# A planned hybrid-decoder kernel: three Strassen-like pairs for four, room behind GpSimd's results, and remainders spread anew

## The chip, the cores and the metric

The kernel runs on one core of a Trainium2 chip, as one launch. The metric is the device time of one execution in microseconds (us). The kernel before was timed three times: 726.03, 728.19 and 728.18 us, a median of 728.18 us. In the profile the engines are PE (TensorE, matmuls), PEld (its weight loads), DVE (VectorE), ACT (ScalarE), POOL (GpSimd) and SP (SyncE, which here only issues transfers).

## What is computed

One decoder layer on 1024 tokens of width 1024, in fp32 (the reference, cut to what matters):

```
mod = silu(c) @ mod_w + mod_b;  shift, scale, gate = split(mod, 3)
h = rmsnorm(x) * (1 + scale) + shift
u = h @ w_in                                  # 1024 x 5120
cv, cg, cs, lx, ls = split(u, 5)              # 1024 columns each
v = causal_depthwise_conv(cv * sigmoid(cg), dw_w, 31 taps)
y_conv = (silu(layernorm(v)) @ pw2_w + pw2_b) * silu(cs)
xs = causal_depthwise_conv(lx, sc_w, 4 taps)
r, i = sigmoid(block_diagonal(xs, wr) + br), sigmoid(block_diagonal(xs, wi) + bi)
a = exp(-8 r softplus(-lam))
hs = scan(h = a h + sqrt(1 - a^2) i xs)       # along the tokens
y_lru = hs * silu(ls)
x = x + (1 + gate) * (concat(y_conv, y_lru) @ w_out)
return rmsnorm(x)
```

## The kernel before

**Tiles.** Everything lies transposed: 128 channels on the partitions, 1024 tokens along the free axis, so that one tile of 128 x 1024 is one of 8 k-tiles of the input or one of 40 column tiles of w_in (i0 to i39 in the tables: conv value, conv gate, conv SiLU gate, lru x, lru gate, 8 each). An fp32 matmul is made of three matmuls of a rounded format: each operand is split into a high part (a cast on ScalarE: whi of weights, uh of tokens) and a remainder (raw minus the high part: wlo, ul), and H x H, H x remainder and remainder x H are summed in PSUM. A column tile is thus 8 k-tiles x 3 terms x 2 halves of 512 tokens = 48 matmuls of 512 columns.

**Who makes a remainder** can be chosen: a subtraction on DVE, one on POOL, or "by transfer": ScalarE writes the negated high part, and an accumulating transfer, which POOL issues, adds the original from memory (the function remainder: ACT, then ADD). For the weights the choice stands in EARLYD, EARLY and LATE (function weights), for the pairs in DENG and WSUB (function duo), for the lru group's result y in YDMA (function gates).

**Pairs.** A slot "iA+iB" of the table ORDER is a pair (function duo, tiles dn and up in PSUM): on four of the eight k-tiles the two column tiles are taken together and computed in the Strassen-Winograd manner, with 7 quarter products for 8. For this the pair needs combinations of its weights (tile wz, four operations of 128 x 256 each, on the engine CSUB, split into wsh and wsl), and sums of the tokens (function token_sums: hx on POOL, split into hhs, by ScalarE, and hls, by POOL), which are made once, before the first pair.

**Stages.** First four column tiles while the input norm is found; then the mixing stage (slots up to 39: a column tile or a pair each, between them the block-diagonal products "gate"; on DVE, ScalarE and GpSimd's transfers the 31 taps of the convolution, on DVE and ScalarE the gates and the scan); slots 40 to 47 the product of the lru group with its half of w_out, also in pairs; then layer norm, the pw2 product, the other half of w_out, the residual and the last norm.

**What sets the order.** A planner (class Plan) takes every operation with an engine, a cost, a priority (mostly the slot number plus or minus something) and what it reads and writes, plays the engines forward in time, and so fixes for each engine one order in which its instructions stand in the program. On the chip each engine goes through its order and waits in place. The planner knows that a DVE operation on two SBUF operands and a POOL operation exclude each other (its "held" times), and counts a latency from an operation's end to its reader (LATENCY: 0.15 us for POOL). Buffers come from a pool of 47 tiles of 128 x 1024 ("big") and are handed on, so that an operation may also wait for the last reader of a buffer's former content. The modulation product is made on DVE: tiles modw of mod_w are multiplied and summed by scalar_tensor_tensor (line 458 of the profile).

**Transfers.** SP issues loads of raw weights and others from its own queue (q1 in the profile), POOL the accumulating ones from another (q0). The residual x is copied from memory to memory (accd <- in_xT, nine transfers) from the slot XCN on, so that later transfers can add to it.

Lines that the prediction names: 439 (ScalarE copies and casts), 447 (ScalarE activations), 458 (scalar_tensor_tensor), 466 (tensor_tensor on DVE or POOL), 471 (POOL's accumulating transfers), 485 (SP's transfers), 599 (matmuls of a column tile), 1329 (gate), 1678 (quarter products of a pair).

Of the kernel before, what the change touches and what calls it, by code (L numbers as in the profile page):

```python
# [31 lines left out]
FIRST = (("in", CG), ("in", CV), ("in", CG + 1), ("in", CV + 1))  # L32
FW = len(FIRST) * P
NEXT = (("in", LS), ("in", CS), ("in", CS + 1))
ORDER = "i10 i24 g0 i2 i25 i11 i3 i26 i33 i12 i4 g1 i34 i23 g2 i13 i35 i5 i27 i21 g3 i14 i19 i6 i36+i28 i15 i30+i37 i7 i29+i38 g4 g6 g5 i31 i39 i22+i18 g7 i20"
EW = FW + len(NEXT) * P
START = ((0, H), (H, T))
END = ((0, H), (H, 768), (768, T))
NBIG = 47
LASTK = 7  # L40
SPARE = 3
# [6 lines left out]
HRES = 0  # L48
POOLED = (1, 3)
TLATE = 3.0  # L50
QGATES = ((1, 5), (3, 0), (3, 2), (3, 4))
# [25 lines left out]
NP = {0: (6,), 512: (6, 0, 7), 768: (6, 0)}  # L77
SUMS = (2, 0, 4, 3, 1, 6, 7, 5)
CSD = 2
SPILL = (0, 2, 4, 6)  # L80
SPP0, SPP1, SPN = 30, 40.5, 41
EVN = 4
CQR = 0
# [5 lines left out]
KQ = -0.3  # L89
TSETS = 15  # L90
DUOA = 2
DUOW = "big"
YSP = (0, 1, 2, 3)
YRES = 5
TSP = 24
TRES = 2
TSUB = "POOL"
WSUB = ("POOL", "POOL", "POOL")
DENG = {14: ("DMA", "DVE", "DVE"), 15: ("POOL", "DMA", "DVE"), 16: ("DMA", "DVE", "POOL"), 17: ("DMA", "DVE", "DMA"), 18: ("POOL", "POOL", "DMA"), 19: ("DVE", "DVE", "POOL"), 20: ("POOL", "DVE", "POOL"), 21: ("DMA", "DMA", "POOL"), 22: ("DVE", "DVE", "DVE"), 23: ("POOL", "DVE", "POOL"), 24: ("POOL", "DVE", "DMA"), 25: ("POOL", "POOL", "DMA"), 26: ("POOL", "POOL", "POOL"), 27: ("POOL", "DMA", "POOL"), 28: ("POOL", "POOL", "DVE"), 29: ("DMA", "DVE", "DVE"), 30: ("DVE", "DVE", "DVE"), 32: ("POOL", "POOL", "POOL"), 34: ("DMA", "DVE", "DVE"), 35: ("DVE", "DVE", "DMA"), 36: ("POOL", "DMA", "DMA"), 37: ("POOL", "DVE", "DVE"), 38: ("DVE", "DVE", "DVE"), 39: ("DMA", "DVE", "DMA"), 40: ("DMA", "DMA", "DVE"), 41: ("DMA", "DMA", "POOL")}
YDMA = (3, 6, 7)  # L100
EVD = 0
DUOE = 1.2
CSUB = "POOL"
LACT = ((0, 0), (0, 1), (1, 0), (1, 1))
LORDER = "p1zy2q3s4r"
LORDERS = {}
# [1 line left out]
LTJ = (0.0, 0.4)  # L108
YORD = (0, 1, 2, 3, 4, 5, 6, 7)
LTDMA = ()  # L110
YSTEP = 0.3
LTD = (2,1)
PREN, PRES = 5, 3
PREP, XCP = 18, 19
PLAND = 6.0
XCN = 35
LEV = ()
LWB = "big"
LWO = 0.7
# [6 lines left out]
STORE_HOLD = ""  # L126
AFTER_ROOT = ((6, 768),)
FORKP = (1, 2, 3)
FORKN = -3.0
FEVD = ()  # L130
FEVN = 0.1
QT = {(0, c): ("HW", "X") for c in "y234"}
PLACED = ("big",)
MARGINS = 2.0
LSN = 1
LEVN = 0.7
# [4 lines left out]
LLATE = 45  # L141
SLOTT = {46: ("HX", "W"), 47: ("HX", "W")}
FINQ = 0.0
LRV = (0, 2, 4)
QRES = 3
SINGLE = (0,)
AHEAD = 4
IDLE, IDLE0 = 12, 4
WARM = (2, 1)
LANDING, MARGIN = 4.0, 2.0  # L150
BACKLOG = 6.0
SP0 = 1.0
# [3 lines left out]
GDOT = "DVE"  # L156
FOLD = "DVE"
EARLY = 18
EARLYD = (14, 28, 30, 31, 32, 33, 38, 40)
LATE, LAND = 41, 6.0  # L160
ISSUE, FLIGHT, RATE = 1.0, 10.0, 3.0
GM = 17
# [30 lines left out]
class Plan:  # L193
# [61 lines left out]
    def order(self):  # L255
# [139 lines left out]
def hymba_layer(ctx: ExitStack, tc: tile.TileContext, xT, vecs, mod_w, w_first, w_in,  # L395
# [31 lines left out]
    def d_cost(n, ptr=0):  # L427
        return 0.07 + 0.00104 * n + 0.06 * ptr
# [33 lines left out]

    def TT(prio, eng, out, a, b, op, n=T, r=(), w=(), reserve=0, after=()):
        e = dve if eng == "DVE" else pool
        return S.op(eng, d_cost(n) if eng == "DVE" else p_cost(n),
                    lambda: e.tensor_tensor(out=out(), in0=a(), in1=b(), op=op), prio, r, w,  # L466
                    reserve=reserve, lock=not in_psum(r), after=after)

# [115 lines left out]

    def weights(s, after=(), n=None, eng=None, where=None, late=(), later=()):
        n = number[s] if n is None else n
        eng = eng or ("DMA" if n in EARLYD or n >= LATE else "POOL" if n < EARLY else "DVE")
        w_bufs(s, where)
        w_slice(s, 0, KT, n - 2.5, n - 1.4, after, eng, late, later)

# [695 lines left out]
    def evac_in(m, ps, n, b=None, rb=(), ev=0.5):  # L1286
# [10 lines left out]
        elif kind == CS:  # L1297
            t = big_buf(f"scs{i}")
            ACT(pr, t, ps, AF.Silu, bias=b, r=[ps, *rb], w=[t])
            scs_d[i] = dram.tile([P, T], F32, tag=f"scs{i}", name=f"scsd{i}")  # L1300
            DMA(pr, lambda: scs_d[i], t, FULL_BYTES, r=[t], w=[("scsd", i)])
        elif kind == LS:
            sls[i] = big_buf(f"sls{i}", parts=2)
            return ACT(pr, sls[i], ps, AF.Silu, bias=b, r=[ps, *rb], w=[sls[i]])
        else:
            xs, xh, xl = (big_buf(f"{a}{i}", d) for a, d in
                          (("xs", F32), ("xsh", F32R), ("xsl", F32R)))

# [734 lines left out]
```

## Time and profile before

| what | before |
|---|---|
| median of three runs | 728.18 us |
| profiled execution | 728.47 us, its span 726.0 us |
| granted TensorE clock, mean | 0.994 |
| TensorE busy | 713.5 us (98%), 3244 matmul records |
| VectorE busy | 655.7 us (90%), 898 |
| ScalarE busy | 474.7 us (65%), 601 |
| GpSimd busy | 206.1 us (28%), 181 |
| transfers | 135.17 MB, mean 186 GB/s |

Views of the profile are read so. A row of engine waits is "engine, tile, line <- what it waited for: us in total, times, longest us". A row of windows gives the stretch, its length, and for PE, PEld, DVE, ACT and POOL the busy us with the count of instructions in brackets, then the granted clock, the share of the transfer engines' time and GB/s; a window asked for one engine and one tile has that one alone. A row of a timeline is start, duration, engine, line, operation, out <- in, shapes, and in square brackets how long the engine stood idle before it and what released it. A row of groups ends in "| busy us, mean ns | idle before, releaser". A row of transfers is out <- in, the issuing queue, the count, KB each, and the median us from issue to landing. Since TensorE is busy nearly always, the other engines matter only where it waits for them.

### The profile page before, as it was taken

The numbers are of one execution on the slowest core, as the hardware profiler recorded it, in microseconds if no ns is written. First come the engines' busy times: TensorE is split into PE (matmuls) and PEld (weight loads), VectorE is DVE, ScalarE is ACT, GpSimd is POOL, SyncE is SP. The second block draws the span as 40 slices with busy tenths as digits, with TensorE's granted clock in tenths as the row PEclk, the third lists the DMA queues.
The fourth block names the chain that finished last, engine by engine and source line by source line (L and its number), as shares of the span: only waits on it lengthen the run. The fifth ranks groups of instructions, "written<-read, shape, count | busy, mean of one in ns | idle before, by whom it ended". The sixth has DMA issues, their size and how long they took to land.

```text
span 726.0 us, 9074 instructions
## 1 busy us (share of the span) xinstructions
PE 713.5 (98%) x3244; PEld 593.0 (82%) x3244; DVE 655.7 (90%) x898; ACT 474.7 (65%) x601; POOL 206.1 (28%) x181
## 2 busy tenths in 40 slices
PE   9999999999989999999999999999999999999996
PEld 8888888888868888888888887878888888888885
DVE  7999999999988989989999999997798966999647
ACT  7650689657659974774676788846797635745322
POOL 0036334433955643075150230011101001100001
PEclk9999999999999999999999999999999999999998
DMA  8946438988788999868743466697947766774006
GB/s 335 407 157 191 65 98 227 233 249 202 179 188 215 240 220 219 216 174 172 169 109 76 152 210 177 221 311 199 259 87 156 185 151 136 234 187 178 30 1 232
DMA packets 44909, 135.17 MB, mean 186 GB/s; under 512 B 5073, under 2 KB 14545, under 8 KB 44753
## 3 DMA queue, kind: packets, MB, share of 16 engines
q1 hardware_dynamic: 27152, 88.95, 34.8%
q0 software_dynamic: 16704, 44.73, 34.4%
q10 hardware_dynamic: 1008, 0.92, 0.4%
q8 instruction: 25, 0.41, 0.2%
q14 instruction: 20, 0.16, 0.1%
HBM read 83.43 MB, written 25.17 MB: 150 GB/s over the span
## 4 chain that ended last, share of the span: by engine, by line
PE 76%; DVE 16%; issue 3%; ACT 3%; DMA 1%; DVEq 0%; POOL 0%; ACTq 0%; POOLq 0%
PE ps L599 25%; PE xout L775 6%; PE xpw L775 6%; PE first L908 5%; DVE caccs L458 5%; PE dn L1678 3%; PE up L599 3%; PE ypw L775 3%; PE lx L1478 3%; DVE xs L458 2%; PE dn L599 2%; DVE cacc L458 2%; PE gate L1329 2%; PE zout L775 1%; PE zpw L775 1%
## 5 line engine op out<-in xcount | busy, mean ns | idle before, releaser
L599 PE MATMUL ps<-uh,whi 128*128 128x512 f32 x448 | 139.1, 392 | 3.6 <-ACT r L447 3.6
L599 PE MATMUL ps<-uh,wlo 128*128 128x512 f32 x448 | 138.4, 390 | 0.0
L599 PE MATMUL ps<-ul,whi 128*128 128x512 f32 x448 | 138.3, 390 | 0.0
L599 PEld LDWEIGHTS ps<-uh,whi 128*128 128x128 f32 x448 | 84.3, 189 | 21.7 <-ACT r L447 4.0
L599 PEld LDWEIGHTS ps<-ul,whi 128*128 128x128 f32 x448 | 84.5, 189 | 17.7
L599 PEld LDWEIGHTS ps<-uh,wlo 128*128 128x128 f32 x448 | 84.4, 188 | 17.6
L439 ACT CAST whi<-raw 128x1024 fp32r<-128x1024 f32 (+1 forms) x44 | 44.3, 1011 | 39.0 <-PE ps L599 15.4
L466 POOL TENSOR_TENSOR wlo<-raw,whi 128x1024 fp32r<-128x1024 f32 (+1 forms) x17 | 44.5, 2628 | 81.4 <-ACT whi L439 81.0
L458 DVE SCALAR_TENSOR_TENSOR cacc<-v,V,cacc 128x511 f32<-128x511 f32 (+14 forms) x90 | 66.8, 743 | 0.8 <-ACT cacc L447 0.5
L458 DVE SCALAR_TENSOR_TENSOR caccs<-v,V,caccs 128x511 f32<-128x511 f32 (+6 forms) x84 | 62.5, 745 | 1.1
L458 DVE SCALAR_TENSOR_TENSOR caccs<-c,wsum,caccs 128x511 f32<-128x511 f32 (+6 forms) x84 | 62.4, 743 | 0.7
L447 ACT ACT_TABLE_LOAD x45 | 57.7, 1283 | 1.7 <-PEq L2035 0.7
L471 POOL DMA_DIRECT2D es<-cq x30 | 30.6, 1030 | 27.9 <-DMA es<-cq 9.1
L458 DVE SCALAR_TENSOR_TENSOR modw<-modw,sc 128x1024 f32<-128x1024 f32 x23 | 37.0, 1611 | 0.0
L471 POOL DMA_DIRECT2D oo<-co x26 | 25.5, 982 | 34.6 <-ACT co L447 12.3
L447 ACT ACTIVATE finsq<-fin 128x512 f32<-128x512 f32 (+2 forms) x14 | 7.9, 570 | 28.7 <-DVE fin L458 15.5
L466 DVE TENSOR_TENSOR wlo<-raw,whi 128x1024 fp32r<-128x1024 f32 (+1 forms) x19 | 23.9, 1259 | 1.2 <-ACT whi L439 1.1
L466 POOL TENSOR_TENSOR o<-fin,bc 128x256 f32<-128x256 f32 (+1 forms) x6 | 4.9, 833 | 70.4 <-ACT bc L439 70.4
L447 ACT ACTIVATE co<-v,V 128x510 f32<-128x510 f32 (+12 forms) x26 | 18.1, 711 | 5.9 <-DVE modw L458 3.6
L471 POOL DMA_DIRECT2D lz<-in_w_out_dram x16 | 14.2, 960 | 26.2 <-ACT lz L447 24.2
L447 ACT ACTIVATE cq<-v,V 128x511 f32<-128x511 f32 (+14 forms) x30 | 21.3, 709 | 0.0
L471 POOL DMA_DIRECT2D accd<-acc x8 | 7.3, 914 | 48.0 <-ACT acc L447 29.1
(515 smaller groups left out, 1926.4 us busy)
## 6 DMA issues: line engine op xcount, KB each, us to landing
raw<-in_w_in_dram SPq DMA_DIRECT2D x36, 512.0 KB, 4.8
modw<-in_mod_w_dram SPq DMA_DIRECT2D x24, 512.0 KB, 7.8
scsd<-scs SPq DMA_DIRECT2D x8, 512.0 KB, 3.4
raw<-in_w_out_dram SPq DMA_DIRECT2D x8, 512.0 KB, 5.9
accd<-acc POOLq DMA_DIRECT2D x8, 512.0 KB, 6.4
rawpw<-in_pw_dram SPq DMA_DIRECT2D x8, 512.0 KB, 4.4
scsr<-scsd SPq DMA_DIRECT2D x8, 512.0 KB, 5.0
rawout<-in_w_out_dram SPq DMA_DIRECT2D x8, 512.0 KB, 3.4
```

The source lines that it names most:

```text
L439: act.copy(out(), in_())
L447: act.activation(out=out(), in_=in_(), func=func, **kw)
L458: dve.scalar_tensor_tensor(out=out(), in0=in0(), scalar=scalar, in1=in1(), op0=op0, op1=op1, accum_out=accum)
L466: lambda: e.tensor_tensor(out=out(), in0=a(), in1=b(), op=op), prio, r, w,
L471: return S.op("POOL", ISSUE, lambda: pool.dma_start(out(), a(), accum_op=ALU.add), prio, r, w, lag=RATE * n / T, after=after, flight=flight)
L599: pe.matmul(ps()[:, a - off:b - off], k3(lhs)()[:, at, :], rhs[k]()[:, a:b], start=(k == first and lhs is wh and rhs is xh and (a - off) % ...
L775: pe.matmul(half(ps, 0)(), half(*lhs)()[:, j * P:j * P + P], half(*rhs)(), start=start and at == 0 and i == 0, stop=at == len(order) - 1 a ...
L908: pe.matmul(ps()[:, a - off:b - off], fw_part(lhs, k, i * P, i * P + P)(), rhs()[:, a:b], start=k == 0 and lhs is wh and rhs is xh, stop=k ...
L1329: pe.matmul(ps()[:, c0:c1], lhs()[:, j, :], rhs()[:, c0:c1], start=st == 0, stop=st == 2)
L1478: pe.matmul(half(ps, h)(), lhs()[:, o:o + P], half(*rhs)(), start=begin and at == 0 and t == 0, stop=at == len(order) - 1 and t == len(ter ...
L1678: pe.matmul(half(ps, h)(), lhs()[:, o:o + P], half(rhs, z)(), start=begin and j == 0 and t == 0, stop=j == NJ - 1 and t == 2, skip_group_c ...
```

## The change

The kernel after is planned from other tables and numbers, and six places of the code let the tables choose what was fixed:

- ORDER: three pairs (i38+i36, i29+i7, i22+i18) in place of four, and another order of the slots.
- PLAG = 1.5: the planner takes the result of a POOL operation (not of its transfers) as ready 1.5 us later for whoever reads it. (PSLOW = 1.0 changes nothing.)
- PGM, PXR, PYM, PXL, PYL: for the named lru tiles the three gate products (xs<-g,xs; xs<-xs,r; sls<-sls,r) and the remainders xsl and yl go to POOL in place of DVE: 3 of each of the first four, and 2 yl (tile 4 stands in YDMA too, which goes first).
- CSUB: the pairs' combinations of weights (wz) go from POOL to DVE: 16 of 128 x 256 on POOL before, 12 on DVE now.
- WE, WSUB, DENG, YDMA: who makes the remainders of weights, pairs and y. By transfer there are now five more of w_in (wlo), one more of a pair's combination (wsl), one less of w_out and one less of y.
- XCN: the copies of x are held to slot 30 in place of 35. The rest are small shifts of priorities and of buffers kept free.

```diff
-ORDER = "i10 i24 g0 i2 i25 i11 i3 i26 i33 i12 i4 g1 i34 i23 g2 i13 i35 i5 i27 i21 g3 i14 i19 i6 i36+i28 i15 i30+i37 i7 i29+i38 g4 g6 g5 i31 i39 i22+i18 g7 i20"
+ORDER = "i24 g0 i10 i2 i11 i3 i26 i25 i12 i4 i33 i34 g2 i35 i21 g1 i13 i5 i27 i14 i20 i6 g3 i30 i37 i19 i28 i15 i38+i36 g6 i29+i7 g5 g4 i31 i39 i22+i18 g7 i23"
...
-DENG = {14: ("DMA", "DVE", "DVE"), 15: ("POOL", "DMA", "DVE"), 16: ("DMA", "DVE", "POOL"), 17: ("DMA", "DVE", "DMA"), 18: ("POOL", "POOL", "DMA"), 19: ("DVE", "DVE", "POOL"), 20: ("POOL", "DVE", "POOL"), 21: ("DMA", "DMA", "POOL"), 22: ("DVE", "DVE", "DVE"), 23: ("POOL", "DVE", "POOL"), 24: ("POOL", "DVE", "DMA"), 25: ("POOL", "POOL", "DMA"), 26: ("POOL", "POOL", "POOL"), 27: ("POOL", "DMA", "POOL"), 28: ("POOL", "POOL", "DVE"), 29: ("DMA", "DVE", "DVE"), 30: ("DVE", "DVE", "DVE"), 32: ("POOL", "POOL", "POOL"), 34: ("DMA", "DVE", "DVE"), 35: ("DVE", "DVE", "DMA"), 36: ("POOL", "DMA", "DMA"), 37: ("POOL", "DVE", "DVE"), 38: ("DVE", "DVE", "DVE"), 39: ("DMA", "DVE", "DMA"), 40: ("DMA", "DMA", "DVE"), 41: ("DMA", "DMA", "POOL")}
-YDMA = (3, 6, 7)
+DENG = {31: ("POOL", "DMA", "DMA"), 37: ("POOL", "DVE", "DVE")}
+YDMA = (4, 5)
...
-CSUB = "POOL"
+CSUB = "DVE"
...
-XCN = 35
+XCN = 30
...
+PLAG, PSLOW = 1.5, 1.0
...
-EARLYD = (14, 28, 30, 31, 32, 33, 38, 40)
+WE = {8: "DMA", 15: "DMA", 25: "DMA", 27: "DMA", 29: "DMA", 30: "DMA", 39: "DMA"}
+PGM, PYM, PXL, PYL, PXR = (3, 5, 7), (0, 5, 7), (3, 4, 7), (1, 2, 4), (4, 5, 6)
...
                 if o.eng == "SP" and o.prio > 0:
                     lat = LANDING if o.prio < 37 else 3.0
+                if o.eng == "POOL" and not o.lag:
+                    lat += PLAG
...
-        eng = eng or ("DMA" if n in EARLYD or n >= LATE else "POOL" if n < EARLY else "DVE")
+        eng = eng or WE.get(n) or ("DMA" if n >= LATE else "POOL" if n < EARLY else "DVE")
...
-            split(pr + 0.2, xh, xl, xs)
+            split(pr + 0.2, xh, xl, xs, eng="POOL" if i in PXL else "DVE")
...
-        TT(pr, "DVE", xs, g, xs, ALU.mult, r=[g, xs], w=[xs])
+        TT(pr, "POOL" if i in PGM else "DVE", xs, g, xs, ALU.mult, r=[g, xs], w=[xs])
...
-        TT(pr, "DVE", xs, xs, r, ALU.mult, r=[xs, r], w=[xs])
+        TT(pr, "POOL" if i in PXR else "DVE", xs, xs, r, ALU.mult, r=[xs, r], w=[xs])
...
-        TT(pr, "DVE", t, t, r, ALU.mult, r=[t, r], w=[t])
+        TT(pr, "POOL" if i in PYM else "DVE", t, t, r, ALU.mult, r=[t, r], w=[t])
...
-            o = split(p, yh[i], yl[i], t, reserve=SPARE)
+            o = split(p, yh[i], yl[i], t, eng="POOL" if i in PYL else "DVE", reserve=SPARE)
```

ScalarE where the casts of the token sums (hhs) stand, with the semaphores that each instruction waits for; r1 is the sigmoid of a gate product, which empties its PSUM tile. First before, then now:

```order
L439 CAST whi17_1743<-raw17_1599 128x1024 [waits DMAHW2_49,PE_49,Pool_49]
L447 ACT_TABLE_LOAD [waits DMASW7_49]
L447 ACTIVATE sig4_1752<-ps15_1652 128x1024 [waits PE_49]
L439 CAST hhs00_1767<-hx00_1671 128x1024 [waits DMAHW6_49,DVE_49,Pool_49]
L439 CAST hhs01_1813<-hx01_1699 128x1024 [waits DMASW1_49,DVE_49,Pool_49]
L439 CAST whi18_1826<-raw18_1701 128x1024 [waits DMAHW4_49,PE_49]
L447 ACTIVATE r1_1838<-gate1_0_1819,V_80 128x1024 [waits PE_49,Pool_49]
```

```order
L451 ACTIVATE r1_2128<-gate1_0_2102,V_80 128x1024 [waits Pool_49]
L451 ACTIVATE g1_2149<-gate1_1_2118,V_80 128x1024 [waits DMAHW3_49,PE_49]
L451 ACT_TABLE_LOAD
L451 ACTIVATE a1_2153<-r1_2128,sp8n_99 128x1024 [waits Activation_49]
L443 CAST hhs01_2173<-hx01_2010 128x1024 [waits DMASW3_49,Pool_49]
L451 ACTIVATE r1_2128<-r1_2128,sp8h_100 128x1024 [waits Activation_49]
```

The cast hhs01 stood ahead of r1 and waited for VectorE (DVE_49) among others; now it stands behind r1 and g1 and waits for a transfer and GpSimd alone.

GpSimd over the token sums of the first two k-tiles (hx00, hx01) and their remainders (hls00, hls01); es and oo are transfers of the convolution. Before, and then now:

```order
L466 TENSOR_TENSOR hx_1671<-hx_1699,hx_1671 128x512
L466 TENSOR_TENSOR wlo_1756<-raw_1599,whi_1743 128x1024
L466 TENSOR_TENSOR hx_1699<-hx_1699,hx_1671 128x512
L471 DMA oo_1060<-co_6_1542 128x505
L466 TENSOR_TENSOR hx_1699<-hx_1699 128x512
L471 DMA es_1503<-cq_2_1555 128x1022
L471 DMA oo_1515<-co_2_1564 128x509
L466 TENSOR_TENSOR hls_1816<-hx_1671,hhs_1767 128x1024
L471 DMA es_1050<-cq_7_1703 128x1017
L466 TENSOR_TENSOR hls_1850<-hx_1699,hhs_1813 128x1024
```

```order
L475 DMA es_1416<-cq_5_1969 128x1019
L470 TENSOR_TENSOR hx_2010<-uh_230,ul_243 128x1024
L475 DMA es_1041<-cq_8_1964 128x1016
L470 TENSOR_TENSOR hx_1730<-hx_2010,hx_1730 128x512
L475 DMA oo_1427<-co_6_1902 128x505
L470 TENSOR_TENSOR hx_2010<-hx_2010,hx_1730 128x512
L470 TENSOR_TENSOR hls_2090<-hx_1730,hhs_2075 128x1024
L470 TENSOR_TENSOR hx_2010<-hx_2010 128x512
L475 DMA es_1041<-cq_9_2047 128x1015
```

The remainder wlo is no longer among them, hls01 comes later, and the transfers stand between; hx00 itself and its first difference (hx_1730) were made further up.

GpSimd and then SP at the first pair of the kernel after (slots 31 and 32), where the nine copies of x now stand:

```order
L475 DMA wlo30_2956<-in_w_in_dram 128x1024
L475 DMA es3_1416<-cq3_14_2979 128x1010
L470 TENSOR_TENSOR wlo31_3021<-raw31_2846,whi31_3016 128x1024
L475 DMA wlo32_3044<-in_w_in_dram 128x768
L475 DMA wsl31_3053<-wz31_2997 128x1024
L470 TENSOR_TENSOR xsl4_3088<-xs4_3019,xsh4_3083 128x1024
```

```order
L489 DMA raw32_2954<-in_w_in_dram 128x1024
L489 DMA cd1_138<-c1_950 128x1024
L489 DMA raw33_3041<-in_w_in_dram 128x1024
L489 DMA accd0_124<-in_xT_dram 128x512
L489 DMA accd1_125<-in_xT_dram 16x8192
L489 DMA accd0_124<-in_xT_dram 128x512
L489 DMA accd2_126<-in_xT_dram 16x8192
L489 DMA accd3_127<-in_xT_dram 16x8192
L489 DMA accd4_128<-in_xT_dram 16x8192
```

In the plan the first copies are issued at the same time as wlo32 and wsl31, which the pair's matmuls read; before, the copies stood at slot 35, with no remainder of a weight by transfer beside them.

More of the change, by code (lines that the diff above doesn't have):

```diff
@@ L40 @@
 LASTK = 7
-SPARE = 3
+SPARE = 2
 SQLAST = 7
@@ L47 @@
 UK = 7
-HRES = 0
+HRES = 1
 POOLED = (1, 3)
@@ L79 @@
 CSD = 2
-SPILL = (0, 2, 4, 6)
+SPILL = (0, 2, 4, 1)
 SPP0, SPP1, SPN = 30, 40.5, 41
@@ L88 @@
 LK = tuple(2 * j + z for z in (0, 1) for j in JS) + tuple(k for k in range(KT) if k // 2 not in JS)
-KQ = -0.3
+KQ = 0
 TSETS = 15
-DUOA = 2
+DUOA = 4
 DUOW = "big"
 YSP = (0, 1, 2, 3)
-YRES = 5
+YRES = 3
 TSP = 24
-TRES = 2
+TRES = 3
 TSUB = "POOL"
 WSUB = ("POOL", "POOL", "POOL")
-DENG = {14: ("DMA", "DVE", "DVE"), 15: ("POOL", "DMA", "DVE"), 16: ("DMA", "DVE", "POOL"), 17: ("DMA", "DVE", "DMA"), 18: ("POOL", "POOL", "DMA"), 19: ("DVE", "DVE", "POOL"), 20: ("POOL", "DVE", "POOL"), 21: ("DMA", "DMA", "POOL"), 22: ("DVE", "DVE", "DVE"), 23: ("POOL", "DVE", "POOL"), 24: ("POOL", "DVE", "DMA"), 25: ("POOL", "POOL", "DMA"), 26: ("POOL", "POOL", "POOL"), 27: ("POOL", "DMA", "POOL"), 28: ("POOL", "POOL", "DVE"), 29: ("DMA", "DVE", "DVE"), 30: ("DVE", "DVE", "DVE"), 32: ("POOL", "POOL", "POOL"), 34: ("DMA", "DVE", "DVE"), 35: ("DVE", "DVE", "DMA"), 36: ("POOL", "DMA", "DMA"), 37: ("POOL", "DVE", "DVE"), 38: ("DVE", "DVE", "DVE"), 39: ("DMA", "DVE", "DMA"), 40: ("DMA", "DMA", "DVE"), 41: ("DMA", "DMA", "POOL")}
-YDMA = (3, 6, 7)
+DENG = {31: ("POOL", "DMA", "DMA"), 37: ("POOL", "DVE", "DVE")}
+YDMA = (4, 5)
 EVD = 0
 DUOE = 1.2
-CSUB = "POOL"
+CSUB = "DVE"
 LACT = ((0, 0), (0, 1), (1, 0), (1, 1))
@@ L110 @@
 LTDMA = ()
-YSTEP = 0.3
+YSTEP = 0.1
 LTD = (2,1)
 PREN, PRES = 5, 3
-PREP, XCP = 18, 19
+PREP, XCP = 18, 15
 PLAND = 6.0
-XCN = 35
+XCN = 30
 LEV = ()
 LWB = "big"
-LWO = 0.7
+LWO = 0.3
 FINP = -0.5
@@ L128 @@
 FORKP = (1, 2, 3)
-FORKN = -3.0
+FORKN = -200
 FEVD = ()
@@ L135 @@
 LSN = 1
-LEVN = 0.7
+LEVN = 0.5
 LWBS = (5, 6, 7)
@@ L143 @@
 FINQ = 0.0
-LRV = (0, 2, 4)
+LRV = (2, 3, 4, 5)
 QRES = 3
@@ L464, in TT @@
         e = dve if eng == "DVE" else pool
-        return S.op(eng, d_cost(n) if eng == "DVE" else p_cost(n),
+        return S.op(eng, d_cost(n) if eng == "DVE" else p_cost(n) * PSLOW,
                     lambda: e.tensor_tensor(out=out(), in0=a(), in1=b(), op=op), prio, r, w,
```

## The prediction

> **What bounds the kernel now.** I read the page's busy row and strip first, then TensorE's waits, then 20-us windows, and went with the chain of waits only into the stretch in which TensorE stood still.
>
> ```profile
> PE 713.5 (98%) x3244; PEld 593.0 (82%) x3244; DVE 655.7 (90%) x898; ACT 474.7 (65%) x601; POOL 206.1 (28%) x181
> PE ps L599 <- ACT r L447: 3.6, 1, 3.6
> PE token_stats L865 <- DVE ones L516: 1.1, 1, 1.1
> PE ly L599 <- DMA wlo<-in_w_out_dram: 0.7, 1, 0.7
> PE dn L1678 <- ACT wk L439: 0.2, 1, 0.2
> 180.00:200.00 20.00, 20.00 (x90) 16.57 (x89) 19.47 (x22) 13.74 (x18) 17.53 (x13) 1.00 0.77 185
> 200.00:220.00 20.00, 16.43 (x66) 13.14 (x65) 16.42 (x16) 12.45 (x14) 9.67 (x8) 0.91 0.90 206
> 440.00:460.00 20.00, 19.80 (x88) 15.99 (x87) 19.94 (x24) 18.52 (x18) 1.75 (x2) 1.00 0.68 197
> 480.00:500.00 20.00, 19.26 (x86) 15.62 (x85) 15.53 (x21) 8.02 (x11) 2.67 (x3) 1.00 0.82 261
> ```
>
> TensorE is busy for 98% of the span, so the count of matmuls sets the time, and anything else matters only as a wait of TensorE. A window without a wait holds 90 matmuls of 512 columns: 20/90 = 0.222 us each. The waits sum to about 6 us, and one is most of it. The window at 200 us holds 66 matmuls in place of 90 at a granted clock of 0.91: 24 x 0.222 = **5.3 us lost at one place**, 3.6 of them idle, the rest matmuls run slowly behind it. The small waits in the last two windows cost 2 and 4 matmuls, 0.4 and 0.9 us. Why it stands there:
>
> ```profile
> 187.76 2.73 POOL L466 TENSOR_TENSOR hx<-uh,ul 128x1024 f32<-128x1024 f32 x1
> 193.95 2.40 POOL L466 TENSOR_TENSOR wlo<-raw,whi 128x1024 fp32r<-128x1024 f32 x1
> 200.55 3.34 POOL L466 TENSOR_TENSOR hls<-hx,hhs 128x1024 fp32r<-128x1024 f32 x1
> 187.59 5.24 DVE L458 SCALAR_TENSOR_TENSOR modw<-modw,sc 128x1024 f32<-128x1024 f32 x1
> 200.29 4.69 DVE L458 SCALAR_TENSOR_TENSOR modw<-modw,sc 128x1024 f32<-128x1024 f32 x1
> 205.07 1.05 ACT L439 CAST hhs<-hx 128x1024 fp32r<-128x1024 f32 x1 [9.99 <-DVE modw L458]
> 206.97 1.11 ACT L447 ACTIVATE r<-gate,V 128x1024 f32<-128x1024 f32 x1
> 208.12 1.17 PE L599 MATMUL ps<-uh,whi 128*128 128x512 f32 x2 [3.57 <-ACT r L447]
> ```
>
> Two VectorE operations on two SBUF operands start beside GpSimd operations of the same kind and end only behind them: 5.24 and 4.69 us, where 1024-element ones take 1.2 alone (row "xs<-xs,r" below). The cast hhs on ScalarE waits 9.99 us for the second, since it is to overwrite that modw's buffer; behind it in ScalarE's order stands sigmoid r, which empties a PSUM tile; TensorE wants that tile.
>
> **The change, part by part.** *Three pairs for four.* A pair takes 7 quarter products for 8 on four of eight k-tiles. The built order has 6 more matmuls of 512 columns: 6 x 0.222 = **+1.33 us**, certain.
>
> *The stall at 204 us.* In the new order hhs01 waits for GpSimd and a transfer, but no longer for VectorE (shown with the change): its buffer is not a modw's. The token sums on GpSimd are spread, with the transfers of the convolution between. The planner now takes the result of a GpSimd operation as ready 1.5 us later, where a meeting adds 0.3 to 0.9 us to one (2.73 and 3.34 against 2.40 alone). So I take the whole loss back: **-5.33**. Bounds: all of it, and 0 if another VectorE operation behind a cluster of GpSimd work does the same (a rival).
>
> *Elementwise work moved to GpSimd.* Rows for 90 to 475 us (VectorE), then the whole span (GpSimd):
>
> ```profile
> L466 DVE TENSOR_TENSOR sls<-sls,r 128x1024 f32<-128x1024 f32 x8 | 11.8, 1475 | 0.1
> L466 DVE TENSOR_TENSOR xs<-g,xs 128x1024 f32<-128x1024 f32 x8 | 10.5, 1318 | 0.9 <-ACT g L447 0.9
> L466 DVE TENSOR_TENSOR xsl<-xs,xsh 128x1024 fp32r<-128x1024 f32 x8 | 10.3, 1286 | 0.0
> L466 DVE TENSOR_TENSOR xs<-xs,r 128x1024 f32<-128x1024 f32 x8 | 9.8, 1219 | 0.1
> L466 DVE TENSOR_TENSOR wlo<-raw,whi 128x1024 fp32r<-128x1024 f32 x15 | 19.6, 1304 | 1.2 <-ACT whi L439 1.1
> L466 DVE TENSOR_TENSOR c<-v 128x512 f32<-128x512 f32 x8 | 5.5, 688 | 0.0
> L466 POOL TENSOR_TENSOR wlo<-raw,whi 128x1024 fp32r<-128x1024 f32 x16 | 42.7, 2677 | 80.2 <-ACT whi L439 79.9 <-PE late L908 0.3
> 90.00:475.00 385.00, 381.24 (x1671) 314.09 (x1671) 371.51 (x465) 287.34 (x336) 152.67 (x125) 1.00 0.75 188
> 90.00:475.00 385.00, 24.72 (x18) 1.00 0.75 188
> ```
>
> VectorE loses 3 each of the first four and 3 net of wlo (fifth row): 3 x (1.48 + 1.32 + 1.29 + 1.22 + 1.30) = 19.8 us. It gains 12 small combinations of weights (128x256), each below the 0.69 us of a 128x512 operation (sixth row): at most 8. GpSimd gains 14 operations at 2.7 (37.8) and loses 2 remainders (5.3) and 16 small combinations: the last row is GpSimd's time on tile wz, 18 records, of which 2 are remainders, 24.7 - 5.3 = 19.4. So GpSimd has 13 us more, VectorE 12 less, of 385. None of it stands on TensorE's path while the order gives room; VectorE is busy for 371.5 of these 385 us, so the relief is real and I count no gain, for outside the stall TensorE lost 0.4 us on that side. The cover is the planned room: in the new order the tightest places in the middle are 7 to 11 matmuls (1.6 to 2.4 us) between producer and reader, where before they were 0 to 8. Taken at **0**; bounds -0.4 (the loss in the window at 440 us gone) and +3.3 (rival three).
>
> The Trainium skill, "GPSIMD Engine Reference", section "Engine selection", would have such work left on VectorE, since two-input elementwise work is about twice as slow on GpSimd; this case's rows agree (2677 against 1304 ns). By that rule alone the 14 moved operations would cost 14 x 1.3 = 18 us of engine time, which no sum here charges to TensorE.
>
> *Remainders by transfer.* A remainder "by DMA" is a negating copy on ScalarE and an accumulating transfer issued by GpSimd. There are 5 more of the input weights and one for a pair's combination (wsl31). What such transfers take:
>
> ```profile
> wlo<-in_w_in_dram POOLq DMA_DIRECT2D x1, 384.0 KB, 7.3
> es<-cq POOLq DMA_DIRECT2D x1, 504.5 KB, 9.1
> wlo<-in_w_out_dram POOLq DMA_DIRECT2D x1, 384.0 KB, 10.7
> oo<-co POOLq DMA_DIRECT2D x1, 253.0 KB, 12.6
> DMA to landing us min/median/max: 5.3/6.3/7.3
> L439 ACT CAST whi<-raw 128x1024 fp32r<-128x1024 f32 (+1 forms) x44 | 44.3, 1011 | 39.0 <-PE ps L599 15.4
> ```
>
> The 9.1 was issued 0.6 us behind the 7.3; the 12.6 was the third of three issued within 1.1 us; the row of three numbers is of the weights' remainders from 300 to 420 us; the last is a cast's 1.01 us. By the order wlo15, 25, 27, 29 and 30 have 34 to 48 matmuls (7.5 to 10.7 us) of room and stand apart from other big transfers: 0. wsl31 is tighter: it is issued right behind wlo32 (GpSimd's order, with the change), when ScalarE has made five more copies and casts after the last matmul of ps29: three of 1.0 and two of three quarters of the size, 0.8 by estimate, together 4.6 us, and about 5.5 with the issue. TensorE has 6 + 48 + 8 = 62 matmuls in that time, 13.8 us: room 8.3. As second of two, issued 1 us later, it should land after 9.1 - 0.6 = 8.5, or up to 9: **+0.5**. Bounds 0 (5.3) and 12.6 - 8.3 = 4.3, plus the clock's share.
>
> *wlo41, at the head of the lru pairs,* is late already (the 10.7 above, 0.7 us of waiting; with the clock's share 0.9). Its first reader now stands 42 matmuls behind the issue, before 45: 3 x 0.222 = **+0.67**. Bounds 0 and 1.3.
>
> *x copies.* Nine transfers from memory to memory on SP's queue are issued five slots earlier, right behind raw33 and just ahead of wlo32. Their readers come after slot 48; the load raw34 queued behind them has over 70 matmuls, 15 us, and one behind the copies landed in 9.2. They cost nothing by themselves; what they do to wsl31 is rival two.
>
> Sum against the profiled span: 726.0 + 1.33 - 5.33 + 0.67 + 0.5 = 723.2. The profiled execution was 728.47, 2.47 more than its span, and the median of the runs is 728.18: 0.3 less. So 728.18 - 2.83 = **725.4 us**.
>
> **The rivals.** *One: more comes back.* wsl31 lands in time, and the loss at the pair of slots 37/38 (window at 440 us, 0.4) goes as well: 725.35 - 0.5 - 0.4 = 724.4; with wlo41 in time too, less 0.67 and 0.9, 722.9. For it: the new order has room where the old had none. Against it: three matmuls less for wlo41.
>
> *Two, on the other side: the x copies hold up wsl31.* In the stretch of the copies before:
>
> ```profile
> 409.26 6.01 SPq L485 DMA_DIRECT2D accd<-in_xT_dram x9
> q1 hardware_dynamic: 433, 3.72, 97.0%
> accd<-in_xT_dram SPq DMA_DIRECT2D x2, 512.0 KB, 12.1
> raw<-in_w_in_dram SPq DMA_DIRECT2D x1, 512.0 KB, 9.2
> csum<-c POOLq DMA_DIRECT2D x1, 512.0 KB, 8.5
> DMA packets 433, 3.72 MB, mean 338 GB/s; under 512 B 126, under 2 KB 126, under 8 KB 338
> ```
>
> From 414 to 425 us SP's queue alone fills 97% of the transfer engines, and 433 - 338 = 95 packets of over 8 KB carry most of its bytes. The one transfer that GpSimd issued then, csum at the end of it, landed after 8.5. If the queues take turns by packet, a small packet of wlo32 or wsl31 waits for a large one each time. Two remainders (0.9 MB) would come with some three times as many bytes of copies, the ratio of the mean packet (3.72 MB over 307 without the tiny ones, 12 KB) to 4 KB: 3.6 MB at 338 GB/s = 10.6 us from wlo32's issue on, with its own issue, 1 us later, at least 9.6 for wsl31 and 1.3 late; by the longest landing above 4.3; at the worst the copies drain first, 409.3 to the last of the 12.1 us landings, some 17 us, 7 late. I take 4.3, and with the slow matmuls behind (1.7 for 3.6 at the stall) 6.3: 725.35 - 0.5 + 6.3 = 731.1. It is slower than before from a cost of 5.5 on, 3.8 us late. Against it: the first copies in the queue are of small rows, and wlo32 goes first.
>
> The Trainium skill, "DMA: Bandwidth & Descriptors", section "Queues, rings and completion order", says that a transfer engine takes turns between queues and drains a whole packet before it switches. It speaks for this rival; no run so far has large packets and GpSimd's transfers together for long enough to show it.
>
> *Three: the meeting of VectorE and GpSimd moves.* GpSimd has 13 us more of such operations; a VectorE operation that meets two in a row ends 4.0 us late (5.24 - 1.2). Where the room is 7 matmuls, 1.6 us, TensorE waits 2.4, with the clock 3.3: 728.7, no change.
>
> *Four: the change doesn't remove the stall,* since hhs01 is late for GpSimd instead: 728.18 + 1.33 + 0.67 + 0.5 = 730.7.
>
> **How the numbers follow.** A measurement tells 0.3%, 2.2 us, from no change: faster is below 726.0, slower above 730.4. The forecast of 725.4 has a chance of 0.45; its own range, 724.2 to 726.8, is for 0.30 below 726.0 and for 0.15 above. Rival one 0.18, all faster. Rival two 0.17: 0.10 slower, 0.07 no change, as wsl31 is over 3.8 us late or less. Rival three 0.13: 0.11 no change, 0.02 slower. Rival four 0.07, slower. So faster 0.48, no change 0.33, slower 0.19. The range, 723.0 to 730.8, takes in rival one to its end, three, and two to its middle.
>
> **What would show it.** Stall gone: every 20-us window from 160 to 400 us holds 90 matmuls at clock 1.00, and TensorE's waits have no row for sigmoid r. wsl31: a row of TensorE's waits "dn <- DMA wsl" says how late it is; under 1 us is the forecast, 4 us rival two. wlo41: the row "ly <- DMA wlo" goes from 0.7 to about 1.4. Rival three would show as a TensorE wait for ScalarE or VectorE with a modw, xsl or sls of over 3 us ahead of it in the chain. The forecast is wrong if the span is above 725 us with no row of a wait over 1 us: then the loss would be in slow matmuls, which I have only behind stalls.

## The result, and the profile after

The changed kernel took **737.14 us** (median of 736.83 to 737.22, 4 runs), the kernel before beside it 727.75 us. The ratio is 1.0133 with a 95% interval of 1.0115 to 1.0150: 1.3% slower. (Two of the 12 executions of the kernel of experiment 6 took 2569 and 3456 us for a cause that no run shows, and are left out of its medians.) The profiled execution had a span of 734.6 us, 8.6 more than before. Busy time and TensorE's waits in the profile after:

```profile
PE 716.0 (97%) x3250; PEld 594.8 (81%) x3250; DVE 649.8 (88%) x891; ACT 475.1 (65%) x601; POOL 219.1 (30%) x181
PE dn L1682 <- DMA wsl<-wz: 6.9, 1, 6.9
PE ly L1482 <- ACT yhs L443: 2.7, 1, 2.7
PE lp L1482 <- DVE acc L462: 0.3, 1, 0.3
```

The rows for sigmoid r (3.6 us) and for wlo41 (0.7) are gone, and two others stand in their place. Windows of 20 us show what each cost:

```profile
180.00:200.00 20.00, 20.00 (x90) 16.53 (x89) 16.38 (x22) 18.54 (x25) 15.24 (x11) 1.00 0.93 203
200.00:220.00 20.00, 20.00 (x90) 16.57 (x89) 19.28 (x28) 12.21 (x16) 6.83 (x8) 1.00 1.06 225
360.00:380.00 20.00, 13.06 (x48) 10.32 (x47) 12.28 (x11) 8.57 (x11) 7.84 (x4) 0.83 0.91 286
480.00:500.00 20.00, 17.01 (x67) 12.58 (x66) 19.71 (x28) 5.57 (x7) 1.77 (x2) 0.91 0.78 256
```

At 200 us there are 90 matmuls again at clock 1.00, where there were 66. At 360 us 42 are missing, 9.3 us: 6.9 of waiting for the pair's remainder wsl31 and the slow matmuls behind it. At 480 us, the head of the lru pairs, 23 are missing, 5.1 us. So 726.0 + 1.33 - 5.33 + 9.3 + 5.1, less the 0.9 that the head of the lru pairs had lost before, is 735.5; the measured span of 734.6 is 0.9 less. Small losses that went may be that difference (the windows at 400, 440 and 660 us had 88 records before, and have 89 to 90).

### The profile page after: what moved, and what is told of

Its sections match the earlier page's. It is cut to its first block, busy times and chain, and to the rows that moved or that the text cites. A ratio compares the mean times of both kernels' runs of the same rounds, so it can differ in the third digit from the quotient of the medians.

```text
span 734.6 us, 9091 instructions
## 1 busy us (share of the span) xinstructions
PE 716.0 (97%) x3250; PEld 594.8 (81%) x3250; DVE 649.8 (88%) x891; ACT 475.1 (65%) x601; POOL 219.1 (30%) x181
## 4 chain that ended last, share of the span: by engine, by line
PE 83%; DVE 8%; ACT 3%; issue 3%; DMA 2%; DVEq 0%; ACTq 0%
PE ps L603 37%; PE xout L779 6%; PE xpw L779 6%; PE first L912 5%; PE ypw L779 3%; PE lx L1482 3%; DMA wsl<-wz 2%; PE gate L1333 2%; PE dn L1682 2%; PE up L603 1%; PE lx L603 1%; PE zout L779 1%; PE zpw L779 1%; DVE caccs L462 1%; PE y L749 1%
## 5 line engine op out<-in xcount | busy, mean ns | idle before, releaser
L603 PE MATMUL ps<-uh,whi 128*128 128x512 f32 x480 | 147.9, 389 | 0.0
L603 PE MATMUL ps<-uh,wlo 128*128 128x512 f32 x480 | 147.8, 389 | 0.0
L603 PE MATMUL ps<-ul,whi 128*128 128x512 f32 x480 | 147.8, 389 | 0.0
L603 PEld LDWEIGHTS ps<-uh,wlo 128*128 128x128 f32 x480 | 90.1, 188 | 18.8
L603 PEld LDWEIGHTS ps<-ul,whi 128*128 128x128 f32 x480 | 90.1, 188 | 18.7
L603 PEld LDWEIGHTS ps<-uh,whi 128*128 128x128 f32 x480 | 89.9, 188 | 18.8 <-ACT g L451 0.2
L470 POOL TENSOR_TENSOR wlo<-raw,whi 128x1024 fp32r<-128x1024 f32 (+1 forms) x16 | 40.4, 2530 | 91.3 <-ACT whi L443 67.6
L475 POOL DMA_DIRECT2D oo<-co x26 | 26.3, 1024 | 23.9 <-DMA oo<-co 8.4
L462 DVE SCALAR_TENSOR_TENSOR modw<-modw,sc 128x1024 f32<-128x1024 f32 x23 | 31.7, 1382 | 0.0
L462 DVE SCALAR_TENSOR_TENSOR xs<-ps,V,xs 128x1023 f32<-128x1023 f32 (+2 forms) x21 | 26.8, 1276 | 0.9 <-ACT xs L451 0.8
L1345 DVE TENSOR_TENSOR_SCAN r<-a,xs 128x1024 f32<-128x1024 f32 x8 | 22.8, 2847 | 0.2 <-POOL xs L470 0.2
```

Source lines behind the costliest of these rows:

```text
L462: dve.scalar_tensor_tensor(out=out(), in0=in0(), scalar=scalar, in1=in1(), op0=op0, op1=op1, accum_out=accum)
L475: return S.op("POOL", ISSUE, lambda: pool.dma_start(out(), a(), accum_op=ALU.add), prio, r, w, lag=RATE * n / T, after=after, flight=flight)
L603: pe.matmul(ps()[:, a - off:b - off], k3(lhs)()[:, at, :], rhs[k]()[:, a:b], start=(k == first and lhs is wh and rhs is xh and (a - off) % ...
L1345: S.op("DVE", 2.2, lambda: dve.tensor_tensor_scan(out=r(), data0=a(), data1=xs(), initial=0.0, op0=ALU.mult, op1=ALU.add), pr, [a, xs], [r])
```

## The two places in the trace

**wsl31.** Two answers about the transfers issued from 358.0 to 358.5 us, and about those under way from 366 to 371 us:

```profile
wsl<-wz POOLq DMA_DIRECT2D x1, 512.0 KB, 14.9
accd<-in_xT_dram SPq DMA_DIRECT2D x1, 512.0 KB, 9.8
wlo<-in_w_in_dram POOLq DMA_DIRECT2D x1, 384.0 KB, 8.3
...
DMA packets 177, 1.68 MB, mean 336 GB/s; under 512 B 47, under 2 KB 47, under 8 KB 137
q1 hardware_dynamic: 86, 1.31, 62.7%
q0 software_dynamic: 91, 0.37, 36.8%
```

wsl31 landed 14.9 us after its issue; TensorE waited the last 6.9, so the room was 8.0. While it was under way SP's queue (q1) moved 40 packets of over 8 KB (177 - 137), which make up its 1.31 MB: about 33 KB each, the rows of the x copies. The other 46 of its 86 packets carry next to nothing (47 packets in all are under 512 B). GpSimd's queue (q0) got 91 packets and 0.37 MB through in these 5 us, 74 GB/s.

**The head of the lru pairs.** GpSimd and VectorE, timelines from 462 us, then the cast and the matmul that wait at the end:

```profile
464.34 2.68 POOL L470 TENSOR_TENSOR yl<-yr,yh 128x1024 fp32r<-128x1024 f32 x1
469.27 2.76 POOL L470 TENSOR_TENSOR sls<-sls,r 128x1024 f32<-128x1024 f32 x1 [1.39 <-DVE r L1345]
472.00 2.85 POOL L470 TENSOR_TENSOR yl<-yr,yh 128x1024 fp32r<-128x1024 f32 x1
...
464.51 4.67 DVE L1345 TENSOR_TENSOR_SCAN r<-a,xs 128x1024 f32<-128x1024 f32 x1
469.11 3.47 DVE L470 TENSOR_TENSOR yr<-yr,yr 128x512 f32<-128x512 f32 x2
472.51 3.42 DVE L470 TENSOR_TENSOR yls<-yr,yhs 128x1024 fp32r<-128x1024 f32 x1
478.73 1.21 DVE L470 TENSOR_TENSOR yls<-yr,yhs 128x1024 fp32r<-128x1024 f32 x1
...
486.23 1.04 ACT L443 CAST yhs<-yr 128x1024 fp32r<-128x1024 f32 x1 [5.56 <-DVE yr L470]
...
487.33 0.79 PE L1482 MATMUL ly<-yhs,lsh 128*128 128x512 f32 x1 [2.73 <-ACT yhs L443]
```

Each of the three VectorE operations on SBUF operands meets a GpSimd operation and ends behind it: the scan in 4.67 us (2.28 for another at 220.80), two yr in 3.47 (0.68 each elsewhere), yls in 3.42 (1.21 a few rows on). That is 2.4 + 2.1 + 2.2 = 6.7 us that VectorE loses in 11, with ScalarE's casts yhs and TensorE's ly waiting behind it. In the kernel before GpSimd issued only transfers at this place, and the scan there took no longer than elsewhere:

```profile
460.64 2.29 DVE L1341 TENSOR_TENSOR_SCAN r<-a,xs 128x1024 f32<-128x1024 f32 x1
```

## The experiments

Times are medians; each ratio is to the kernel before, timed beside the experiment, with a 95% interval.

**1. The packets of the x copies.** The copies' rows cut from 32 KB to 4 KB by a padded target; the order on every engine is unchanged.

```diff
-        acc_d[m] = dram.tile([P, T], F32, tag=f"acc{m}", name=f"accd{m}")
+        acc_d[m] = dram.tile([P, T + 16], F32, tag=f"acc{m}", name=f"accd{m}")[:, :T]
```

> The changed kernel with one difference: the seven whole copies of x from memory to memory go in rows of 4 KB (128 x 1024) where they went in rows of 32 KB (16 x 8192). Bytes, order on every engine and issue times stay. Theory (the transfer engines take turns by packet, and a small packet of wlo32 or wsl31 waits for a 32 KB one each time): wsl31, which landed 14.9 us after its issue, lands after 8 to 10, TensorE's wait at dn falls from 6.9 to 0 to 2 us, and the time from 737.1 to 728.5 to 731. Rival (it is the backlog: whatever SP has queued goes ahead, by bytes): wsl31 stays at 14 to 15 and the time within 1 us of 737.1.

Measured: 732.41 us, ratio 1.0073 (1.0050 to 1.0095). wsl31's landing, TensorE's wait for it, and the transfers under way from 364 to 367 us:

```profile
DMA to landing us min/median/max: 11.3/11.3/11.3
PE dn L1682 <- DMA wsl<-wz: 3.4, 1, 3.4
q0 software_dynamic: 130, 0.46, 77.6%
q1 hardware_dynamic: 133, 0.31, 29.9%
```

Beside small packets GpSimd's queue moved 0.46 MB in 3 us, 153 GB/s for 74 beside large ones, and the two queues got nearly as many packets through (130 and 133; in the changed kernel 91 and 86 in the 5 us above). The size of the packets is worth 3.6 us of wsl31's landing and some 4.7 us of time. But 11.3 is not the 8 to 10 expected: the copies cost something by their bytes too.

**2. The copies later.** XCN back from 30 to 35.

```diff
-XCN = 30
+XCN = 35
```

> The changed kernel with the copies of x held to slot 35 again, as before; everything behind slot 30 is planned anew with that. Theory (the copies are what delays wsl31): it lands after 8.5 to 9.5 us, TensorE waits 0 to 1.5 us there, 728 to 730.5, if nothing at slot 35 takes the copies' part; the loss at the lru pairs stays. Rival (two remainders in a row are late without the copies too): wsl31 after over 11 us, a wait of over 3 us, 732 or more.

Measured: 735.67 us, ratio 1.0102 (1.0084 to 1.0120). wsl31 and TensorE's waits:

```profile
DMA to landing us min/median/max: 8.5/8.5/8.5
PE dn L1682 <- DMA wsl<-wz: 0.5, 1, 0.5
PE ly L1482 <- DVE c L470: 3.7, 1, 3.7
PE dn L1682 <- ACT up L443: 2.5, 1, 2.5
PE dn L1682 <- DVE up L470: 1.0, 1, 1.0
PE gate L1333 <- ACT sls L451: 1.0, 1, 1.0
```

Without the copies beside it wsl31 lands after 8.5 us and the wait is 0.5. So, by one profile of each kernel, of 14.9 us 8.5 are there without the copies, 2.8 come with the copies' bytes and 3.6 with the size of their packets. The time hardly falls, for the order planned anew behind slot 30 has other waits of 1 to 3.7 us. The sentence "if nothing takes the copies' part" was the one that failed.

**3. wsl31 made by VectorE.**

```diff
-DENG = {31: ("POOL", "DMA", "DMA"), 37: ("POOL", "DVE", "DVE")}
+DENG = {31: ("POOL", "DMA", "DVE"), 37: ("POOL", "DVE", "DVE")}
```

> The changed kernel with the remainder wsl31 of the first pair made by VectorE, not by transfer; everything behind it is planned anew with that. Theory (the wait at dn31 is the transfer's alone): no wait for wsl31, about 8.8 us less (6.9 idle and 1.9 of slow matmuls behind): 728 to 729, with the loss at the head of the lru pairs as it was (2.9 us of waiting). Rival (the pair is short of time there whoever makes it): another wait of over 2 us at dn, 731 or more.

Measured: 728.50 us, ratio 1.0000 (0.9989 to 1.0012). The wait for wsl31 is gone; 0.8 us is left at that pair (dn <- DVE up). The time fell by 8.6 us, as the theory had it. At the lru pairs, where yl and sls stay on GpSimd, the order is planned anew as well: the wait for yhs is down to 0.5, and one for wlo41's transfer takes its place ("ly L603 <- DMA wlo", 2.2 us).

**4. yl and sls back on VectorE**, at the head of the lru pairs alone.

```diff
-PGM, PYM, PXL, PYL, PXR = (3, 5, 7), (0, 5, 7), (3, 4, 7), (1, 2, 4), (4, 5, 6)
+PGM, PYM, PXL, PYL, PXR = (3, 5, 7), (0, 5), (3, 4, 7), (), (4, 5, 6)
```

> The changed kernel with the remainders yl of the lru tiles 1, 2 and the product sls of tile 7 back on VectorE, so that GpSimd has no elementwise operation in the last 20 us ahead of the lru pairs. Only the order from there on changes. Theory (a scan of 4.67 us for 2.3, and yr, yls of 3.4 us for 1.2 to 1.4, beside three GpSimd operations made yhs late): the wait of ly for yhs (2.7 us) and its slow matmuls go, 737.1 falls by 3 to 4.6, to 732.5 to 734. Rival (VectorE is simply short there, the three operations cost it 3.6 us of its own): the wait stays at 2 to 4 us, 736.5 to 738.5.

Measured: 736.32 us, ratio 1.0111 (1.0095 to 1.0127). Neither theory: the wait for yhs is gone, and wlo41, which it had covered, is waited for in its place:

```profile
PE dn L1682 <- DMA wsl<-wz: 6.8, 1, 6.8
PE ly L603 <- DMA wlo<-in_w_out_dram: 3.4, 1, 3.4
```

**5. The whole head of the lru pairs**: the edit of 4, and wlo41 on VectorE; wsl31 stays by transfer. (LRV names the remainders of w_out that VectorE makes, counted from wlo40. It is one of the tables of the change: before it was (0, 2, 4).)

```diff
-LRV = (2, 3, 4, 5)
+LRV = (1, 2, 3, 4, 5)
```

> The changed kernel with the head of the lru pairs alone mended: yl of tiles 1 and 2, sls of tile 7 and the remainder wlo41 on VectorE; wsl31 stays by transfer beside the copies. Theory (the two heads are separate and add): the wait of 6.8 us for wsl31 stays, no wait over 0.5 us at the lru pairs, 737.1 less 4.6 (the matmuls that the window at 480 us lost): 732 to 733.5. Rival (the lateness at the lru pairs comes from the long wait at dn31, which shifts the engines against each other): a wait of over 2 us stays there, 735 or more.

Measured: 732.28 us, ratio 1.0051 (1.0034 to 1.0069): 4.9 less than the changed kernel, while wsl31 still costs 6.7 us of waiting. One wait at the lru pairs is left, 0.7 us for acc, over the 0.5 of the theory. The two places add to within 1 us: the spans of 3 and 5 are 7.4 and 4.9 below the changed kernel's, that of 8, with both edits, 12.8.

**6. Both transfers on VectorE**: the edits to DENG (3) and LRV (5), with yl and sls left on GpSimd.

> The changed kernel with two remainders on VectorE that went by transfer: wsl31 of the first pair, and wlo41 at the head of the lru pairs (LRV with 1). Theory (both heads wait only for these transfers): against the run with wsl31 alone moved (728.5), the wait of 2.2 us for wlo41 and its slow matmuls go and nothing takes their place: 725 to 726.5, with 1 to 2 us of small waits left. Rival (VectorE is late at the head of the lru pairs, and its lateness stands behind the transfer's): a wait for yhs or yls of over 1.5 us, 727.5 to 729.

Measured: 724.94 us, ratio 0.9946 (0.9929 to 0.9962). The same kernel again:

> The kernel with wsl31 and wlo41 on VectorE once more, for a profile (the first one was of a disturbed execution). Theory: TensorE waits for no transfer; span 722 to 723.5; at the head of the lru pairs at most 1 us of waits for yhs, yls or acc. Rival: a wait of over 1.5 us there, made up by none of the others.

Measured: 724.88 us, ratio 0.9959 (0.9946 to 0.9972), span 722.5:

```profile
PE dn L1682 <- DVE up L470: 0.8, 1, 0.8
PE lx L1482 <- ACT yhs L443: 0.6, 1, 0.6
PE lx L1482 <- DVE yls L470: 0.4, 1, 0.4
```

No wait for a transfer is left. What is left at the lru pairs, 1.0 us, goes when GpSimd's yl and sls go (8).

**7. With the copies in rows of 4 KB as well** (edits of 6 and 1).

> The same kernel (wsl31 and wlo41 on VectorE) with the copies of x in rows of 4 KB. wlo32 is then the only transfer that GpSimd issues beside the copies, and it has about 20 us of room (its first reader stands in the pair's last quarter). Theory (a packet's size matters only to a transfer that is short of room): no difference, within 1 us of the run without. Rival (the copies' large packets hold up the loads behind them too): 1 to 2 us faster; or, since 4 KB packets move fewer bytes in a turn, the loads of raw weights behind the copies come later and it is 1 to 2 us slower.

Measured: 725.19 us, ratio 0.9960 (0.9948 to 0.9972): no difference from 724.88. Where no transfer of GpSimd's is short of room beside the copies, the size of their packets made no difference.

**8. With yl and sls on VectorE as well** (edits of 6 and 4).

> The same kernel (wsl31 and wlo41 on VectorE) with yl of the lru tiles 1 and 2 and sls of tile 7 on VectorE as well. Theory (VectorE is late at the head of the lru pairs only by what it loses beside GpSimd): the small waits there go, 0.5 to 1.5 us faster than 725.3. Rival (VectorE is full there; 3.6 us more of its own work): 0.5 to 2.5 us slower than 725.3.

Measured: 724.66 us, ratio 0.9963 (0.9950 to 0.9976), span 721.8. The waits for yhs and yls are gone from the trace; in time it can't be told from 6. This is the version with the fewest waits: 0.4% faster than the kernel before, 1.7% faster than the changed one.

**9. The room alone.** The kernel before, with the 1.5 us in its planner and nothing else of the change.

```diff
+                if o.eng == "POOL" and not o.lag:
+                    lat += 1.5
```

> The kernel before with one part of the change alone: the planner takes a GpSimd operation's result as ready 1.5 us later. Four pairs, the old table and the old engines stay; the whole order is planned anew. In that order hhs01 stands behind the sigmoid r1. Theory (the room is what takes the stall away): no wait of 3 us near 204 us, 728.1 less 5.3 less or more some small waits, 722 to 725. Rival (it was the new table of slots that moved hhs01 away, and room alone makes waits elsewhere): 727 to 731.

Measured: 739.99 us, ratio 1.0158 (1.0134 to 1.0182). Neither theory: it is 9 us above the rival's range too. The stall at 204 us is not gone but longer, though hhs01 stands behind r1 now:

```profile
197.97 2.76 POOL L468 TENSOR_TENSOR hx<-hx 128x512 f32<-128x512 f32 x1
199.82 4.18 POOL L468 TENSOR_TENSOR hls<-hx,hhs 128x1024 fp32r<-128x1024 f32 x1
203.51 2.78 POOL L468 TENSOR_TENSOR hx<-uh,ul 128x1024 f32<-128x1024 f32 x1
...
201.12 6.25 DVE L460 SCALAR_TENSOR_TENSOR modw<-modw,sc 128x1024 f32<-128x1024 f32 x1
207.52 1.23 DVE L468 TENSOR_TENSOR v<-ps,sig 128x1024 f32<-128x1024 f32 x1
...
208.84 1.11 ACT L449 ACTIVATE r<-gate,V 128x1024 f32<-128x1024 f32 x1 [7.04 <-DVE v L468]
...
208.80 1.22 PE L601 MATMUL ps<-uh,whi 128*128 128x512 f32 x2 [4.92 <-DVE v L468]
```

modw meets two 1024-element operations of GpSimd in a row and takes 6.25 us; v, which empties a PSUM tile, stands behind it, and both the sigmoid r1 and TensorE itself wait for v: 7.04 and 4.92 us, where TensorE had waited 3.57. In this order the same meeting reaches TensorE through v, in the old one through hhs01 and r1. The window at 200 us holds 58 matmuls (66 before). The rest of the loss lies elsewhere: 27 matmuls are missing in the window at 320 us, and 4 to 8 in four windows behind it.

**10. The change without the room.**

```diff
-PLAG, PSLOW = 1.5, 1.0
+PLAG, PSLOW = 0.0, 1.0
```

> The changed kernel with the 1.5 us of room taken away again (0), everything else of the change kept. Theory (the room takes the stall away): the token sums and casts meet VectorE again, a TensorE wait of 2 to 4 us between 160 and 260 us comes back. Rival (the new table and buffers do): 90 matmuls in each window there, as in the changed kernel, and only the waits behind slot 30 differ.

Measured: 740.91 us (one run). The windows at 180 and 200 us hold 90 matmuls each at clock 1.00, as in the changed kernel. The waits come later:

```profile
PE ly L603 <- DMA wlo<-in_w_out_dram: 3.3, 1, 3.3
PE ps L603 <- DMA wlo<-in_w_in_dram: 3.1, 1, 3.1
PE dn L1682 <- DVE up L470: 3.0, 1, 3.0
PE dn L1682 <- POOL wsl L470: 2.2, 1, 2.2
```

The 3.1 is wlo30, which landed after 11.8 us beside copies of x. So the room is not what took the stall at 204 us away; the rest of the change did, its tables, engines and buffers together. In the changed kernel GpSimd issues only transfers from 198.1 to 222.4 us, and the two modw that fall there meet nothing (1.22 and 1.21 us). The first:

```profile
201.74 1.22 DVE L462 SCALAR_TENSOR_TENSOR modw<-modw,sc 128x1024 f32<-128x1024 f32 x1
```

From 300 us on the kernel without the room waits in more places, and its one execution took 3.8 us longer than the changed kernel: the room seems of use there, which one execution doesn't prove.

**11. A fourth pair again**, in the kernel of 8.

```diff
-ORDER = "... g3 i30 i37 i19 ..."
+ORDER = "... g3 i30+i37 i19 ..."
```

> The kernel with wsl31, wlo41, yl and sls on VectorE (724.7) and a fourth pair again: i30 and i37 as one, slots 26 and 27. Theory (a pair is worth its 6 matmuls where its combinations and copies find room): 6 x 0.222 = 1.3 us less, 723 to 724. Rival (a pair's copies between its quarters, ScalarE's and VectorE's, stand in the way: its order has four places with no matmul between producer and reader): 0.5 to 4 us more, 725 to 729.

Measured: 738.97 us, ratio 1.0136 (1.0118 to 1.0154), 14.3 us more than without (about 13 when each is set against the kernel before beside it):

```profile
PE up L1682 <- ACT up L443: 6.4, 2, 6.1
PE dn L1682 <- DVE up L470: 2.5, 2, 1.3
PE ps L603 <- DVE v L470: 2.4, 1, 2.4
```

The new pair's quarters wait for ScalarE's copies between them. ScalarE had lost 6.42 us at 299.90 in the chain of waits to a store (scsd <- scs) whose buffer it was to reuse. Three pairs in place of four cost 1.3 us of matmuls; a fourth at this place cost some ten times as much.

## Why the prediction was wrong, by its own steps

- **Three pairs, +1.33:** borne out as far as it shows. TensorE has 6 more records, and the sum without the two late places, 726.0 + 1.33 - 5.33 = 722.0, is near the span of the mended kernel (721.8), which has 0.9 us of waiting at a pair that the sum leaves out. It was not timed alone; experiment 11 shows that where a pair stands counts for more.
- **The stall at 204 us, -5.33:** right in size and sign, wrong in its reason. I gave the loss to hhs01's buffer and the gain to the room. With the room alone TensorE's wait there grew from 3.6 to 4.9 us (9), and without the room it stayed away (10). In both kernels with the stall VectorE's modw meets a run of GpSimd operations ahead of the sigmoid; in both without it GpSimd only issues transfers there. Which of the change's many differences parts them was not taken apart, so this step came out right by luck.
- **Elementwise work on GpSimd, 0:** right in the stretch from 160 to 360 us, which has no wait of TensorE. Wrong at the head of the lru pairs, the step that I priced by wlo41 alone (+0.67): there are yl, sls and yl on GpSimd in the last 10 us, and VectorE lost 6.7. Rival three was this mechanism, with 3.3 us at a place in the middle; the measured term is 5.1 - 0.9 = 4.2 us, at the head of a stage. It belongs to these operations in this order, not to their engine alone: in 3 and 6 the same three stay on GpSimd in an order planned anew, TensorE waits 0.9 to 1.0 us for what stands behind them, and taking them away (8) bought nothing that can be measured. GpSimd's busy time grew by 13.0 us, as worked out (13); VectorE's fell by 5.9 in place of 12, the longer operations at this head among the reasons. wlo41 was late as well, hidden behind yhs until experiment 4 took its cover away: 3.4 us there, where 1.4 was forecast.
- **wsl31, +0.5:** the step that failed. Both of its sizes were right: the room was 8.0 (8.3 worked out), and without the copies the transfer landed after 8.5 (8.5, closer than an estimate from one row of another transfer could promise) and TensorE waited the 0.5. What I left out of the sum was the copies' part, 6.4 us more, and with the clock's share the term was 9.3. Rival two named the mechanism and the place, with a chance of 0.17 and 6.3 us. Its worst bound, 7 us late when the copies drain first, was nearly the measurement. I had argued it down with the copies' small first rows and wlo32's place ahead; but the first large packets were through before wlo32's first one (nine from 360 to 361 us, with none of GpSimd's), wlo32 itself took 8.3 us, and wsl31 went beside the six large copies.

So the time lies 6 us above the range because the two lateness terms came together, with rival two at its worst bound: 725.35 - 0.5 + 9.3 - 0.67 + 4.2 = 737.7, against 737.14. I had priced each rival alone. wsl31's term alone would have passed the range's end of 730.8; experiment 5, which has it nearly alone, took 732.28. The Trainium skill, "DMA: Bandwidth & Descriptors", section "Queues, rings and completion order", has a transfer engine take turns between queues by whole packets. The runs agree in kind: by the trace's own packets, GpSimd's queue and SP's got 130 and 133 through where both queues' are small, 91 and 86 beside the large ones, and half the bytes per us there. Whether the page's packet, a group of descriptors, is what the trace counts as one, no run here shows; nor whether SP's 46 nearly empty packets took a turn each.

One size in the prediction is a little small throughout. The timelines have matmuls 0.227 us apart (482.63 to 483.99 us in six steps), for a window of 20 us counts the matmuls cut by both its ends, and 20/90 = 0.222 divides by them. All terms counted in matmuls are some 2% larger so, 9.5 us for wsl31 in place of 9.3, and no reading changes.

## What to carry to other kernels

A remainder or load that is due soon and goes through one queue must be priced with what the other queue moves in those microseconds, its bytes and the size of its packets (here 2.8 and 3.6 us of one landing); "behind nothing in its own queue" is not enough. Where one stage hands over to the next, price every engine's last 10 us with the GpSimd operations that VectorE will meet there, since a wait that ends last there covers the next one (yhs covered wlo41). And a planner's constant that is meant for one stall moves the whole order (alone, this one cost 12 us): try it alone before it is given credit.

## What the runs showed that I had not expected

GpSimd's accumulating transfers run at very different rates: 0.43 MB in 2 us, 215 GB/s, with no other queue busy (362 to 364 us of experiment 2), 153 GB/s beside small packets, 74 GB/s beside packets of 32 KB. A VectorE operation that met two GpSimd operations in a row lasted up to 6.25 us, where the same one alone took 1.22.
